# Turning the activations between two layers: from TensorE's transposes to VectorE's 32x32 blocks and GpSimd's transfers

## The chip, the cores and the metric

The kernel runs on one core of a Trainium2 chip. The metric is the device time of one execution in microseconds (us); the time before is the median of three executions. One execution was also recorded by the hardware profiler, and all rows shown here come from such recordings.

## The reference

Two layers, each a mixer over 256 tokens of width 2048, followed by a residual and a layer norm. Cut to what matters here:

```python
def hybrid_layer(x, mem, w_in, ..., w_mem_kv, w_out, ln_g, ln_b):
    h = x @ w_in                        # (256, 2048) @ (2048, 6672)
    a_q, a_k, a_v, a_z, b_q, b_k, b_v, b_z, b_lr, m_q, m_z = split(h)
    y_a = chunk_band_attention(a_q, a_k, a_v, rel_table)
    y_b = gla_chunk_recurrence(b_q, b_k, b_v, gates(b_lr)) ...
    mk, mv = split(mem @ w_mem_kv)      # keys and values of 256 memory tokens
    y_m = memory_attention(m_q, mk, mv)
    y = concatenate([y_a * silu(a_z), y_b * silu(b_z), y_m * silu(m_z)])
    return layer_norm(DEEPNORM_ALPHA * x + y @ w_out, ln_g, ln_b)

def reference(...):
    h = x
    for l in range(2):
        h = hybrid_layer(h, mem, w_in[l], ..., ln_g[l], ln_b[l])
    return h
```

The output of layer 0, normed, is the `x` of layer 1. The products need it with the model dimension on the partitions (turned), since TensorE sums over partitions. The residual of layer 1 needs it with the tokens on the partitions (not turned).

## The kernel before

**Products.** A group of columns of a weight matrix is computed by `as_group`: eight pieces of weights (128 x 2 x 512 float32, 512 KB), and for each piece twelve matmuls (two blocks of 128 model rows, two halves of the tokens, three products). Each float32 operand is split in two parts that TensorE takes at full rate: `parts` has ScalarE cast the high part (`hi`, line 128) and VectorE subtract it to get the low part (`lo`, line 129). For a block and a half, `as_products` multiplies in this order: high activations by high weights, low activations by high weights, high activations by low weights. The activations are the operand that is loaded into the array (LDWEIGHTS), the weights stream.

**Buffers.** `piece` takes its buffers `raw`, `wh` and `wl` from a ring of four: piece n+4 goes into the place of piece n. The turned activations lie in four quarters `xq[0..3]`, each an `operand()` of 128 x 4 blocks x (high, low) x 256 tokens, from a ring of five; quarter q serves the pieces 2q and 2q+1 of a group.

**Order.** TensorE, SyncE and GpSimd run in the order in which the program is written. For ScalarE and VectorE a scheduler decides the order when the kernel is built: the casts of weight pieces have a high priority (`tc.high_priority(AHEAD)`), and `placed_here` keeps an instruction where the program has it relative to its neighbours. Work that is to lie between the products is a Python generator: `tick()`, called after each piece, advances those in `active` and `side`; an entry of `side` starts at a given tick.

**Between the layers.** `norm_between` norms the whole output of layer 0, `res` (128 tokens x 2 halves x 2048), in place without gain and bias: ScalarE takes the column blocks 0 and 2, VectorE 1 and 3 (four instructions each). Meanwhile TensorE runs the first group of layer 1, the values of the memory (called MV here), which does not need `res`. Then comes the group of the memory's keys (MK), also without `res`, and then the queries and keys of the linear attention (BQK), the first group on the new activations; after it the first group of values (V). `transposed`, a generator that is run during MK, turns `res`: eight times four transposes of 128 x 128 on TensorE into a PSUM bank, a gain and bias per model row on the way out (ScalarE one block, VectorE the other), and `parts`. The gain and bias come turned as well: `norm_columns` loads them as 32 rows, and one transpose turns these into `gbT`. `restored` later applies gain and bias to `res` itself for the residual.

**Turning without TensorE.** The kernel has another way, `turned`, used for attention operands: VectorE transposes each 32 x 32 block in place of a 128 x 512 tile (line 525), GpSimd writes the tile to a buffer `home` in device memory (line 527), and four reads per tile (line 532) bring the blocks to their partitions. The reads are put on GpSimd's queue two ticks later.

Of the kernel before, what the change touches and what calls it, by code (L numbers as in the profile page):

```python
# [8 lines left out]
F32 = mybir.dt.float32  # L9
# [3 lines left out]
AF = mybir.ActivationFunctionType  # L13
ALU = mybir.AluOpType
# [4 lines left out]
P = 128  # L19
D = 2048  # L20
T = 256
# [11 lines left out]
AHEAD = 4000  # L33
# [3 lines left out]
def hybrid_trunk_kernel(  # L37
# [7 lines left out]
    pe, dve, act, pool, sp = nc.tensor, nc.vector, nc.scalar, nc.gpsimd, nc.sync  # L45
# [4 lines left out]
    waiting, active, side, done, now, linear = [], [], [], set(), [0], []  # L50

    def tick(share=1.0):

        now[0] += share
        for e in [e for e in side if e[1] <= now[0]]:
            side.remove(e)
            after = next(e[0], None)
            if after is not None:
                side.append((e[0], now[0] + after))
            else:  # L60
                done.add(e[0])
        while True:
            while waiting and len(active) < (3 if all(g in done for g in linear) else 2):
                active.append((waiting.pop(0), 0))
            due = [e for e in active if e[1] <= now[0]]
            if not due:
                return
            active.remove(due[0])
            g = due[0][0]
            after = next(g, None)  # L70
            if after is not None:
                active.append((g, now[0] + after))
                return
            done.add(g)

    def finish(gens):
        while not all(g in done for g in gens):
            tick()

    def enter(name, bufs=1, **kw):  # L80
        return ctx.enter_context(tc.tile_pool(name=name, bufs=bufs, **kw))
# [5 lines left out]
    hd = enter("hd", 1)  # L87
# [5 lines left out]
    drm = enter("drm", 6, space=bass.MemoryType.DRAM)  # L93
# [3 lines left out]
    def nm(s):  # L97
        uid[0] += 1
        return f"{s}_{uid[0]}"
# [4 lines left out]
    def bank():  # L104
        return psa.tile([P, 512], F32, name=nm("bk"), tag="bk")

    def scratch(shape, dtype=F32):
        return sc.tile(shape, dtype, name=nm("sc"), tag="sc")
# [4 lines left out]
    ident = cst.tile([P, P], F32, name="ident")  # L113
# [3 lines left out]
    def operand():  # L117

        x = opp.tile([P, 4, 2, T], F32R, name=nm("x"), tag="x")
        return x[:, :, 0], x[:, :, 1], x.rearrange("p j h t -> p j (h t)")  # L120
# [5 lines left out]
    def parts(hi, lo, src, keep=lambda ins: ins):  # L126

        keep(act.copy(hi, src))  # L128
        keep(dve.tensor_tensor(lo, src, hi.bitcast(F32), op=ALU.subtract))  # L129
# [477 lines left out]
        act.copy(y, po[:, :256])  # L607
        yield 2

    def transposed(xq, gbT):  # L610

        raw, gT = gbT
        pt = bank()
        pe.transpose(pt[:, :P], raw, ident)
        dve.tensor_copy(gT, pt[:, :32])
        for q in range(4):
            x = operand()
            hi, lo, _ = x
            xq.append(x)
            for j in range(0, 4, 2):  # L620
                pt = bank()
                y = scratch([P, 2, T])
                for jj in range(2):
                    kt = q * 4 + j + jj
                    for t in range(2):
                        pe.transpose(pt[:, jj * T + t * P:jj * T + (t + 1) * P], res[:, t, kt * P:(kt + 1) * P], ident)  # L626
                with tc.high_priority(AHEAD // 4):
                    for jj in range(2):
                        kt = q * 4 + j + jj
                        src, g, b = pt[:, jj * T:(jj + 1) * T], gT[:, kt:kt + 1], gT[:, 16 + kt:17 + kt]  # L630
                        if jj == 0:
                            act.activation(y[:, jj], src, AF.Identity, bias=b, scale=g)
                        else:
                            dve.tensor_scalar(y[:, jj], src, g, b, op0=ALU.mult, op1=ALU.add)
                    parts(hi[:, j:j + 2], lo[:, j:j + 2], y)
                yield 1

    def restored(gb):

        for n in range(WO_N):  # L640
            for t in range(2):
                r = res[:, t, columns(n)]
                tc.keep_in_program_order(dve.tensor_tensor(r, r, gb[n][0], op=ALU.mult))
                dve.tensor_tensor(r, r, gb[n][1], op=ALU.add)
                yield 2

    def columns(n):
        return slice(n * 512, (n + 1) * 512)
# [31 lines left out]
    def norm_columns(l):  # L680

        raw = hd.tile([P, P], F32, name=nm("gbrow"), tag="pairs0")
        pool.memset(raw, 0.0)
        for i, src in enumerate((ln_g, ln_b)):
            pool.dma_start(raw[i * 16:i * 16 + 16], src[l].rearrange("(k p) -> k p", p=P))
        return raw, hd.tile([P, 32], F32, name=nm("gbT"), tag="pairs1")

    def norm_rows(l, rows):

# [104 lines left out]
    res = per.tile([P, 2, D], F32, name="res")  # L794
# [3 lines left out]
    for l in range(L):  # L798
# [15 lines left out]
        xq = []  # L814
        if l == 0:
            def each(p):
                if p in (2, 4, 6, 7):
                    xq.append(resident_quarter(len(xq), xT[len(xq)]))

            raw = hd.tile([P, 4, T], F32, name=nm("qk"), tag="qk", bufs=4)  # L820
            laid_out(first_memory(mv, each), raw, lambda src, at: parts(at(mk[0]), at(mk[1]), src, placed_here))
        else:
            memq = []
            parts(*mv, as_group(w512[l, G_MV], memq, 512, 2, memT))
            gens = [transposed(xq, gbT), restored(gb)]
            waiting.append(gens[0])
            raw = hd.tile([P, 4, T], F32, name=nm("qk"), tag="qk", bufs=4)
            mkey = staged(G_MK, memq, raw, lambda src, at: parts(at(mk[0]), at(mk[1]), src, placed_here))
            finish(gens[:1])

        gq = hd.tile([P, 2, T], F32, name=nm("gq"), tag="gq")
        gk = hd.tile([P, 2, T], F32, name=nm("gk"), tag="gk")
        raw = hd.tile([P, 4, T], F32, name=nm("qk"), tag="qk", bufs=4)
# [7 lines left out]
        qk = scratch([P, 2, 256])  # L841
# [2 lines left out]
        dg = small([P, 8], "ms")  # L844
        dve.tensor_reduce(dg, qk.rearrange("p t (h d) -> p (t h) d", d=64), AX.X, ALU.add)
        if l > 0:
            waiting.append(gens[1])
        gp = gla_inputs(l)
        if l == 0:
            sp.dma_start(ident, ident_d)  # L850
# [20 lines left out]
        blocks = scratch([P, 2, 64])  # L871
        dve.transpose(blocks.rearrange("p b (t j) -> p t b j", j=32), lr[:, :, :64].bitcast(F32).rearrange("p t (b j) -> p t b j", j=32))
        home = drm.tile([P, 2, 64], F32, name=nm("home"), tag="home64")
# [15 lines left out]
        bias = {}  # L889
# [11 lines left out]
        gens = [[gla(*gp, gq, gk, lrT, dg, asv, yraw)]]  # L901
# [12 lines left out]
        for half in range(2):  # L914
            q, k = (hd.tile([P, 4, T], F32, name=nm("qk"), tag="qk", bufs=4) for _ in range(2))
# [43 lines left out]
        gb = []  # L959
# [8 lines left out]
        for n in range(WO_N):  # L968
# [3 lines left out]
            src = wo_pieces(l, n)  # L972
            if last and n == WO_N - 1:
# [3 lines left out]
                rest = bank()[:, :256]  # L977
# [39 lines left out]
        if not last:  # L1017
            for n in range(WO_N):
                both = per.tile([P, 2, 512], F32, name=nm("gb"), tag=f"yr{n}")
                gb.append((both[:, 0], both[:, 1]))  # L1020
                load_norm(n)
            norm_between(stats)
            gbT = norm_columns(l)


# [84 lines left out]
```

## Time and profile before

| | |
|---|---|
| median of 3 executions | 900.3 us (900.08 to 900.83) |
| the profiled execution's own time | 900.78 us |
| its span in the trace | 899.0 us |
| granted TensorE clock, mean | 0.998 |
| TensorE busy | 891.3 us (99%) |
| VectorE, ScalarE, GpSimd busy | 611.8, 478.6, 214.4 us |
| transfers | 213.74 MB, mean 238 GB/s |

The profiled execution's time lies 1.8 us over its span; these 1.8 us lie around the span and are not touched by the change. A timeline row has the start in us from the span's start, the length in us, the engine, the line of the kernel, the operation with output and input, and the count; behind it in brackets the time that the engine sat idle before it and what ended that. Rows with a count above 1 merge neighbours; one instruction's length overlaps the next one's start on an engine, so the cost of an instruction on a busy engine is the distance between starts.

### The profile page before, as it was taken

Reading aid. Unit: us, or ns where it says so; the run is one execution under the profiler, and the core shown is the slowest. Engines: PE = TensorE matmul, PEld = TensorE weight load, DVE = VectorE, ACT = ScalarE, POOL = GpSimd, SP = SyncE. Lnnn points to the kernel's source line nnn. Section 1 sums busy time; section 2 is a strip of 40 time slices with the busy share of each in tenths; the row PEclk is TensorE's granted clock in tenths of the full one; section 3 lists DMA queues with packets and bytes.
Section 4 is the critical chain, followed back from the end, with each engine's and each line's share of the span. In section 5 each row is a group of like instructions: output and inputs, shape, how many; then the busy total and the mean of one; then the engine's idle time right before and its main releaser. Section 6 shows DMA issues by size and latency. Waiting matters only on the chain.

```text
span 899.0 us, 13806 instructions
## 1 busy us (share of the span) xinstructions
PE 891.3 (99%) x4687; PEld 746.6 (83%) x4687; DVE 611.8 (68%) x887; ACT 478.6 (53%) x686; POOL 214.4 (24%) x401
## 2 busy tenths in 40 slices
PE   9999999999999999999999999999999999999997
PEld 7888988888988888888888888888888888888885
DVE  6756568767477667665587777796565767676766
ACT  6644575555445566544476444854744457565440
POOL 0022103115315443410000221231061344433200
PEclk9999999999999999999999999999999999999999
DMA  8887779867989797975675859697479897979762
GB/s 309 310 260 226 231 235 268 262 207 220 275 254 241 236 271 238 316 236 188 227 241 184 233 164 286 195 292 213 150 224 296 244 270 221 287 217 289 218 183 94
DMA packets 164838, 213.74 MB, mean 238 GB/s; under 512 B 24752, under 2 KB 142896, under 8 KB 164768
## 3 DMA queue, kind: packets, MB, share of 16 engines
q1 hardware_dynamic: 148256, 173.29, 63.4%
q0 software_dynamic: 16224, 39.18, 15.2%
q8 instruction: 37, 0.61, 0.3%
q10 hardware_dynamic: 288, 0.39, 0.1%
q14 instruction: 33, 0.27, 0.1%
HBM read 193.20 MB, written 19.53 MB: 237 GB/s over the span
## 4 chain that ended last, share of the span: by engine, by line
PE 98%; DMA 1%; DVE 0%; ACT 0%; SPq 0%; issue 0%
PE acc L102 91%; PE bk L102 6%; DMA raw<-w 1%; PE bk L626 0%; ACT res L784 0%; SPq L179 0%; ACT wh L128 0%; DVE stats L770 0%; DVE res L769 0%; SPq L203 0%; SPq L201 0%; DVE res L720 0%; DVE mvt L723 0%; PE bk L773 0%; ACT nparts L774 0%
## 5 line engine op out<-in xcount | busy, mean ns | idle before, releaser
L102 PE MATMUL acc<-wh,x 128*128 128x512 f32 (+2 forms) x2516 | 749.4, 381 | 0.4 <-ACT wh L128 0.2
L102 PEld LDWEIGHTS acc<-wh,x 128*128 128x128 f32 x2516 | 460.7, 188 | 87.0 <-ACT wh L128 1.3
L129 DVE TENSOR_TENSOR wl<-raw,wh 128x1024 fp32r<-128x1024 f32 (+3 forms) x321 | 368.2, 1151 | 209.5 <-ACT wh L128 204.9
L128 ACT CAST wh<-raw 128x1024 fp32r<-128x1024 f32 (+3 forms) x321 | 318.7, 996 | 346.6 <-PE acc L102 212.8
L102 PE MATMUL acc<-wl,x 128*128 128x512 f32 (+2 forms) x1258 | 476.6, 379 | 0.0
L102 PEld LDWEIGHTS acc<-wl,x 128*128 128x128 f32 x1258 | 236.2, 188 | 45.6 <-DVE wl L129 1.1
L527 POOL DMA_DIRECT2D home<-sc x70 | 39.2, 560 | 458.1 <-DVE sc L525 442.6
L532 POOL DMA_DIRECT2D pT<-home x96 | 52.5, 553 | 28.5 <-DMA home<-sc 12.8
L532 POOL DMA_DIRECT2D qk<-home x64 | 34.9, 553 | 30.4 <-DMA home<-sc 28.5
L532 POOL DMA_DIRECT2D zT<-home x48 | 26.2, 552 | 21.8 <-DMA home<-sc 14.0
L525 DVE STREAM_TRANSPOSE sc<-sc 128x512 f32<-128x512 f32 (+1 forms) x38 | 24.9, 667 | 3.7 <-ACT sc L950 3.0
L532 POOL DMA_DIRECT2D yr<-home x48 | 26.3, 555 | 3.2 <-DMA home<-sc 3.2
L525 DVE STREAM_TRANSPOSE sc<-acc 128x512 f32<-128x512 f32 x28 | 18.3, 691 | 5.0 <-PE acc L102 4.8
L554 ACT ACTIVATE sc<-sc,mx 128x128 f32<-128x128 f32 (+1 forms) x32 | 14.4, 449 | 13.0 <-DVE mx L552 13.0
L547 DVE SCALAR_TENSOR_TENSOR sc<-bk,bias 128x384 f32<-128x384 f32 x16 | 8.6, 538 | 10.7 <-PE bk L102 10.7
L128 ACT CAST x<-sc 128x512 fp32r<-128x512 f32 x20 | 12.3, 617 | 5.0 <-DVE sc L508 3.8
L129 DVE TENSOR_TENSOR x<-sc,x 128x512 fp32r<-128x512 f32 x20 | 13.7, 685 | 1.4 <-ACT x L128 1.4
L102 PEld LDWEIGHTS bk<-pT,asv 128*128 128x128 f32 x64 | 11.8, 189 | 1.8
L102 PE MATMUL bk<-qk,qk 128*128 128x128 f32 (+1 forms) x64 | 13.1, 326 | 0.0
L102 PE MATMUL bk<-pT,asv 128*128 128x256 f32 (+1 forms) x64 | 13.0, 326 | 0.0
L659 DVE SCALAR_TENSOR_TENSOR res<-res,acc 128x512 f32<-128x512 f32 x15 | 9.7, 681 | 4.0 <-PE acc L102 4.0
L129 DVE TENSOR_TENSOR x<-raw,x 128x1024 fp32r<-128x1024 f32 x5 | 6.1, 1226 | 8.9 <-ACT x L128 8.8
(204 smaller groups left out, 506.4 us busy)
## 6 DMA issues: line engine op xcount, KB each, us to landing
raw<-w SPq DMA_DIRECT2D x387, 256.0 KB, 4.7
raw<-w SPq DMA_DIRECT2D x62, 512.0 KB, 4.9
home<-sc POOLq DMA_DIRECT2D x54, 256.0 KB, 4.3
raw<-w SPq DMA_DIRECT2D x32, 388.0 KB, 5.1
raw<-w SPq DMA_DIRECT2D x32, 264.0 KB, 3.3
qk<-home POOLq DMA_DIRECT2D x64, 64.0 KB, 5.2
raw<-w SPq DMA_DIRECT2D x32, 124.0 KB, 4.8
bias<-relw SPq DMA_DIRECT2D x16, 192.0 KB, 4.6
```

The costliest lines, as they stand in the source:

```text
L102: pe.matmul(o, l, r, start=start, stop=stop, skip_group_check=True)
L128: keep(act.copy(hi, src))
L129: keep(dve.tensor_tensor(lo, src, hi.bitcast(F32), op=ALU.subtract))
L525: dve.transpose(blocks.rearrange(order, j=32), src.rearrange("p (g b j) -> p g b j", b=4, j=32))
L527: pool.dma_start(homes[-1], blocks)
L532: pool.dma_start(dst[b * 32:(b + 1) * 32], home[:, b].rearrange("(a i) n -> i a n", a=4))
L547: dve.scalar_tensor_tensor(s, pb[:, :384], SCALE, bias[h], op0=ALU.mult, op1=ALU.add)
L554: act.activation(s[:, own[t]], s[:, own[t]], AF.Exp, bias=mx[:, t:t + 1], accum_out=zs[:, t:t + 1])
L659: dve.scalar_tensor_tensor(r, r, ALPHA, acc, op0=ALU.mult, op1=ALU.add)
```

## The change

`transposed` is gone, and with it all 32 transposes of `res` and the one of the gain and bias on TensorE. Right after `norm_between`, four calls of `turned` bring the whole of `res` through VectorE's blocks and `home` buffers to four tiles `xT`: eight block transposes on VectorE, eight writes and thirty-two reads on GpSimd's queue. `norm_columns` turns the gain and bias in the same way, with one block transpose, one write and four reads, while the output projection of layer 0 still runs. A new generator `landed` takes the place of the rest of `transposed`: gain and bias, now read from `xT`, then `parts`. It is put on `side` six ticks after MV's end, one step per tick, two steps to a quarter, with all its instructions `placed_here` and without the raised priority. The program no longer finishes the generator before BQK.

```diff
-    def transposed(xq, gbT):
-
-        raw, gT = gbT
-        pt = bank()
-        pe.transpose(pt[:, :P], raw, ident)
-        dve.tensor_copy(gT, pt[:, :32])
-        for q in range(4):
-            x = operand()
-            hi, lo, _ = x
-            xq.append(x)
-            for j in range(0, 4, 2):
-                pt = bank()
-                y = scratch([P, 2, T])
-                for jj in range(2):
-                    kt = q * 4 + j + jj
-                    for t in range(2):
-                        pe.transpose(pt[:, jj * T + t * P:jj * T + (t + 1) * P], res[:, t, kt * P:(kt + 1) * P], ident)
-                with tc.high_priority(AHEAD // 4):
-                    for jj in range(2):
-                        kt = q * 4 + j + jj
-                        src, g, b = pt[:, jj * T:(jj + 1) * T], gT[:, kt:kt + 1], gT[:, 16 + kt:17 + kt]
-                        if jj == 0:
-                            act.activation(y[:, jj], src, AF.Identity, bias=b, scale=g)
-                        else:
-                            dve.tensor_scalar(y[:, jj], src, g, b, op0=ALU.mult, op1=ALU.add)
-                    parts(hi[:, j:j + 2], lo[:, j:j + 2], y)
-                yield 1
+    def landed(x, xT, q, gT):
+
+        hi, lo, _ = x
+        xv = xT.rearrange("p t a (k j) -> p k t a j", j=32)
+        for j in range(0, 4, 2):
+            y = scratch([P, 2, T])
+            for jj in range(2):
+                kt = q * 4 + j + jj
+                src, g, b = xv[:, j + jj], gT[:, kt:kt + 1], gT[:, 16 + kt:17 + kt]
+                o = y[:, jj].rearrange("p (t a j) -> p t a j", t=2, j=32)
+                if jj == 0:
+                    placed_here(act.activation(o, src, AF.Identity, bias=b, scale=g))
+                else:
+                    placed_here(dve.tensor_scalar(o, src, g, b, op0=ALU.mult, op1=ALU.add))
+            parts(hi[:, j:j + 2], lo[:, j:j + 2], y, placed_here)
+            yield 1
...
-        return raw, hd.tile([P, 32], F32, name=nm("gbT"), tag="pairs1")
+        gT = hd.tile([P, 32], F32, name=nm("gbT"), tag="pairs1")
+        blocks = scratch([P, 4, 32])[:32]
+        dve.transpose(blocks, raw[:32].rearrange("p (b j) -> p b j", j=32))
+        home = drm.tile([32, 4, 32], F32, name=nm("home"), tag="home32")
+        pool.dma_start(home, blocks)
+        for b in range(4):
+            pool.dma_start(gT[b * 32:(b + 1) * 32], home[:, b])
+        return gT
...
             parts(*mv, as_group(w512[l, G_MV], memq, 512, 2, memT))
-            gens = [transposed(xq, gbT), restored(gb)]
-            waiting.append(gens[0])
+            gens = [restored(gb)]
+
+            def rest():
+                for q, xT in turns.items():
+                    xq.append(operand())
+                    yield from landed(xq[q], xT, q, gbT)
+
+            side.append((rest(), now[0] + 6))
             raw = hd.tile([P, 4, T], F32, name=nm("qk"), tag="qk", bufs=4)
             mkey = staged(G_MK, memq, raw, lambda src, at: parts(at(mk[0]), at(mk[1]), src, placed_here))
-            finish(gens[:1])
...
             norm_between(stats)
             gbT = norm_columns(l)
+            turns = {}
+            for q in range(4):
+                turns[q] = hd.tile([P, 2, 4, P], F32, name=nm("xT"), tag="qk", bufs=4)
+                turned(P, *((turns[q][:, t], res[:, t, columns(q)]) for t in range(2)))
```

How this moves instructions shows at two places. The first is VectorE between the layers, at the end of MV. In the kernel before, `wl_4399` is the low part of MV's last piece, and `wl_4421`, `wl_4454`, `wl_4483` those of MK's pieces 0, 1 and 2:

```order
L678 TENSOR_SCALAR res<-res,rstd_4220,nmr_4221 128x512 x4
L129 TENSOR_TENSOR wl_4399<-raw_4397,wh_4398 128x1024
L129 TENSOR_TENSOR wl_4421<-raw_4419,wh_4420 128x1024
L129 TENSOR_TENSOR wl_4454<-raw_4452,wh_4453 128x1024
L129 TENSOR_TENSOR wl_4483<-raw_4481,wh_4482 128x1024
```

The same place in the changed kernel, where `wl_4475` is the low part of MV's last piece and `wl_4497` that of MK's piece 0:

```order
L667 TENSOR_SCALAR res<-res,rstd_4220,nmr_4221 128x512 x4
L129 TENSOR_TENSOR wl_4475<-raw_4473,wh_4474 128x1024
L525 STREAM_TRANSPOSE sc_4255<-res 128x4x4x32
L525 STREAM_TRANSPOSE sc_4259<-res 128x4x4x32
L525 STREAM_TRANSPOSE sc_4264<-res 128x4x4x32
L525 STREAM_TRANSPOSE sc_4268<-res 128x4x4x32
L525 STREAM_TRANSPOSE sc_4273<-res 128x4x4x32
L525 STREAM_TRANSPOSE sc_4277<-res 128x4x4x32
L525 STREAM_TRANSPOSE sc_4282<-res 128x4x4x32
L525 STREAM_TRANSPOSE sc_4286<-res 128x4x4x32
L129 TENSOR_TENSOR wl_4497<-raw_4495,wh_4496 128x1024
```

All eight block transposes now stand between the low parts of MV's last piece and of MK's first.

The second place is ScalarE in BQK. In the kernel before, `x_4618` is the last quarter of the activations (each cast fills one half of it), `sc_4649` what the gain and bias of its second half made, and `wh_4736`, `wh_4755`, `wh_4774`, `wh_4793`, `wh_4812` are the high parts of BQK's pieces 3 to 7:

```order
L128 CAST wh_4736<-raw_4735 128x1024
L128 CAST x_4618<-sc_4620 128x2x256
L632 ACTIVATE sc_4649<-bk_4648,gbT_4245 128x256
L128 CAST wh_4755<-raw_4754 128x1024
L128 CAST x_4618<-sc_4649 128x2x256
L128 CAST wh_4774<-raw_4773 128x1024
L128 CAST wh_4793<-raw_4792 128x1024
L128 CAST wh_4812<-raw_4811 128x1024
```

In the changed kernel `x_4727` is the third quarter and `x_4776` the last; `wh_4807`, `wh_4826` and `wh_4845` are BQK's pieces 5, 6 and 7, and `wh_4893` and `wh_4918` the pieces 0 and 1 of the next group, V:

```order
L128 CAST wh_4807<-raw_4806 128x1024
L621 ACTIVATE sc_4728<-xT_4272,gbT_4245 128x256
L621 ACTIVATE sc_4752<-xT_4272,gbT_4245 128x256
L128 CAST wh_4826<-raw_4825 128x1024
L128 CAST x_4727<-sc_4728 128x2x256
L128 CAST x_4727<-sc_4752 128x2x256
L128 CAST wh_4845<-raw_4844 128x1024
L128 CAST wh_4893<-raw_4892 128x1024
L128 CAST wh_4918<-raw_4917 128x1024
L621 ACTIVATE sc_4777<-xT_4281,gbT_4245 128x256
L621 ACTIVATE sc_4801<-xT_4281,gbT_4245 128x256
L128 CAST x_4776<-sc_4777 128x2x256
```

The cast of the last quarter's first half has moved from behind the weight cast of BQK's piece 3 to behind that of V's piece 1, six weight casts later.

More of the change, by code (lines that the diff above doesn't have):

```diff
@@ L846, in hybrid_trunk_kernel @@
         if l > 0:
-            waiting.append(gens[1])
+            waiting.append(gens[0])
         gp = gla_inputs(l)
```

## The prediction

> **What bounds the kernel now.** I read the page first: its busy times (part 1) and the chain of work that ended last (part 4).
>
> ```profile
> PE 891.3 (99%) x4687; PEld 746.6 (83%) x4687; DVE 611.8 (68%) x887; ACT 478.6 (53%) x686; POOL 214.4 (24%) x401
> PE 98%; DMA 1%; DVE 0%; ACT 0%; SPq 0%; issue 0%
> ```
>
> TensorE is the bound. Then the waits of TensorE, in whole:
>
> ```profile
> PE bk L102 <- DVE eps L797: 1.1, 1, 1.1
> PE bk L773 <- DVE nt L738: 0.9, 1, 0.9
> PE bk L102 <- ACT nparts L774: 0.3, 1, 0.3
> PE acc L102 <- ACT wh L128: 0.2, 1, 0.2
> ```
>
> The first is the start of the kernel, the next two its end, so between the ends TensorE never waits for anybody. Two things follow: every matmul taken out shortens the kernel by its place on TensorE, and every wait put into the middle lengthens it in full. VectorE and ScalarE have time to spare in sum; what counts is whether one operand is late at one moment.
>
> **What is removed.** The timeline of TensorE around the transposes:
>
> ```profile
> 467.20 0.62 PE L102 MATMUL acc<-wh,x 128*128 128x512 f32 x2
> 467.65 0.39 PE L102 MATMUL acc<-wl,x 128*128 128x512 f32 x1
> ...
> 469.92 0.27 PE L614 MATMUL bk<-ident,gbrow 128*128 128x128 f32 x1
> 470.03 0.60 PE L626 MATMUL bk<-ident,res 128*128 128x128 f32 x4
> ...
> 473.23 0.60 PE L626 MATMUL bk<-ident,res 128*128 128x128 f32 x4
> 473.59 0.71 PE L102 MATMUL acc<-wh,x 128*128 128x512 f32 x2
> ...
> 495.72 0.62 PE L102 MATMUL acc<-wh,x 128*128 128x512 f32 x2
> ...
> 498.44 0.61 PE L102 MATMUL acc<-wh,x 128*128 128x512 f32 x2
> ...
> 509.32 0.62 PE L102 MATMUL acc<-wh,x 128*128 128x512 f32 x2
> ```
>
> MK starts at 467.20, and its third matmul, the first that takes a low weight part, at 467.65. A piece without transposes takes 498.44 - 495.72 = 2.72 us. From 469.92 to 495.72 lie eight pieces and all 33 transposes: 25.80 - 8 x 2.72 = **4.04 us** that go. A lower bound counts only the four transposes' own places, 473.59 - 473.23 = 0.36 us: 8 x 0.36 + 0.11 = 2.99 us. I take 4.04, since the pieces between are slower (their matmuls follow at a slightly larger distance) than those outside.
>
> The Trainium skill, page VectorE: DVE Perf Modes, section Rules for kernel authors, speaks against the change: a 128x128 transpose belongs on TensorE where a PSUM destination will do, with 390 ns for it. Worked out from that page, an estimate of the gain would be 33 x 0.39 = 12.9 us; the trace disagrees, since 33 cost 4.04 us there.
>
> **What is added on VectorE: a wait at MK's first piece.** VectorE and ScalarE at the end of MV, and the distance between two block transposes elsewhere:
>
> ```profile
> 459.67 1.92 DVE L678 TENSOR_SCALAR res<-res,rstd,nmr 128x512 f32<-128x512 f32 x4
> 461.50 1.22 DVE L129 TENSOR_TENSOR wl<-raw,wh 128x1024 fp32r<-128x1024 f32 x1
> 463.57 3.50 DVE L129 TENSOR_TENSOR wl<-raw,wh 128x1024 fp32r<-128x1024 f32 x3 [0.86 <-ACT wh L128]
> ```
>
> ```profile
> 459.67 2.93 ACT L676 ACTIVATE res<-res,nmr,rstd 128x512 f32<-128x512 f32 x4
> ```
>
> ```profile
> 359.86 1.31 DVE L525 STREAM_TRANSPOSE sc<-sc 128x512 f32<-128x512 f32 x2 [0.69 <-ACT sc L950]
> 361.09 0.72 DVE L508 TENSOR_TENSOR sc<-zT,yr 128x256 f32<-128x256 f32 x2
> ```
>
> Before, the low parts of MK's pieces 0 to 2 start at 463.57. Now the eight block transposes come first. They can start when MV's last low part is through, 461.50 + 1.22 - 0.08 of overlap = 462.64 (the norm's last block is done at 459.67 + 2.93 = 462.60). Two took 361.09 - 359.86 = 1.23 us, so eight take 4.92, to 467.56; the low part takes 1.22, to 468.78. TensorE wants it at 467.65. The wait sits at the load of the activations that goes with this matmul, and that load is then no longer hidden:
>
> ```profile
> L102 PEld LDWEIGHTS acc<-wh,x 128*128 128x128 f32 x2516 | 460.7, 188 | 87.0 <-ACT wh L128 1.3
> ```
>
> With its 0.19 the matmul starts at 468.97: a wait of **1.3 us**, 1.1 without the load. Queued behind the transposes are also the low parts of pieces 1 to 3; each takes 1.2 against TensorE's 2.72, so they catch up. SyncE's refill of the raw ring starts up to 4 us later, and lands within
>
> ```profile
> DMA to landing us min/median/max: 2.7/4.5/9.8
> ```
>
> in the median 4.5 us (min, median and max of the loads of weight pieces), at about 474, while MK's piece 4 is due at 467.20 + 1.3 + 4 x 2.72 = 479.4. At the longest landing, 9.8, piece 4 would be about 1.5 us late; I count nothing and keep this for the range.
>
> **What is added on GpSimd: hidden.** Its queue gets 8 writes, then 32 reads.
>
> ```profile
> 366.99 4.36 POOL L532 DMA_DIRECT2D zT<-home  x8 [3.75 <-DMA home<-sc]
> ...
> 373.72 0.55 POOL L963 DMA_DIRECT2D gb<-ln_g  x1 [1.25 <-DMA zT<-home]
> ```
>
> ```profile
> home<-sc POOLq DMA_DIRECT2D x54, 256.0 KB, 4.3
> zT<-home POOLq DMA_DIRECT2D x48, 64.0 KB, 5.8
> ```
>
> Eight reads are issued in 4.36 us, and a further transfer then waited for an old one to land, so I take 5.8 + 0.5 us per eight. The last block transpose ends at 467.6; its write is issued by 468.2 and lands 4.3 later, at 472.5. The first quarter's last read follows and lands by 479, the others 6.3 us apart: 485, 491, 498. ScalarE asks for the first when MK's piece 7 is cast, near 480, and BQK needs it at 467.20 + 1.3 + 8 x 2.72 = 490.3. The fourth is asked for near 508. Everything lands in time, with 6 us or more to spare for TensorE. MK's own turning is queued behind these reads on GpSimd, but starts only at 490.
>
> The gain and bias are turned during layer 0's output projection, where VectorE idles about 1.5 us per piece and is three pieces ahead: nothing, and at worst under 1 us.
>
> **What is moved on ScalarE: a wait in BQK.** The cast of the last quarter now stands behind that of V's piece 1. When is that one made?
>
> ```profile
> 489.27 1.05 ACT L128 CAST wh<-raw 128x1024 fp32r<-128x1024 f32 x1 [1.18 <-PE acc L102]
> 490.22 0.61 ACT L128 CAST x<-sc 128x512 fp32r<-128x512 f32 x1
> 490.74 0.56 ACT L632 ACTIVATE sc<-bk,gbT 128x256 f32<-128x256 f32 x1
> ...
> 509.30 1.06 ACT L128 CAST wh<-raw 128x1024 fp32r<-128x1024 f32 x1 [1.15 <-PE acc L102]
> ```
>
> ```profile
> 491.49 0.69 DVE L129 TENSOR_TENSOR x<-sc,x 128x512 fp32r<-128x512 f32 x1
> ```
>
> The ring has four places, so V's piece 1 takes that of BQK's piece 5 and is cast when TensorE is through with it: the row at 509.30, where BQK's piece 6 starts at 509.32. Piece 6 is the first that needs the last quarter. So when TensorE reaches piece 6, ScalarE begins: the cast 0.95 (490.22 - 489.27), two gain-and-bias instructions 0.47 each (0.56 less the 0.09 by which rows overlap), the quarter's high cast 0.61: 2.5 us. Then VectorE's low part 0.69, and 0.19 for the load: the second matmul starts 3.4 us after the first should have, against 0.23 normally. A wait of **3.2 us**; 2.6 if low part and loads were hidden, 3.6 with 0.1 for each handover. The third quarter has the same form, but stands behind the cast of BQK's piece 6, which is made at the end of piece 2; its low part is ready 0.95 + 0.61 + 1.23 + 0.05 = 2.84 us later, and TensorE wants it 2.72 + 0.23 = 2.95 later, load included: **0.1 us**, at most 0.3.
>
> **The sum.** -4.04 + 1.3 + 0.1 + 3.2 = +0.6 us on the profiled execution's 900.78, which is 901.4; that execution lies 0.48 over the median of 900.3, so the forecast is **900.9 us**. With the bounds of the terms it runs from -4.04 + 1.1 + 2.6 = -0.3 to -2.99 + 1.4 + 0.3 + 3.6 = +2.3, 900.0 to 902.6. What can be told from no change here is about 0.2%, 1.8 us; below 898.5 is faster, above 902.1 slower.
>
> **The rivals.** *The clock falls in the wait (slower).* The timeline of TensorE at the end of the kernel, and busy times in short stretches (the number after POOL's is the granted clock):
>
> ```profile
> 893.54 0.39 PE L102 MATMUL bk<-gbrow,nparts 8*128 8x512 f32 x1
> ```
>
> ```profile
> 893.00:894.00 1.00, 0.94 (x3) 0.45 (x3) 0.75 (x3) 0.50 (x1) 0.00 (x0) 1.00 0.37 131
> 895.70:895.90 0.20, 0.00 (x0) 0.00 (x0) 0.00 (x0) 0.00 (x0) 0.00 (x0) 1.00 1.04 389
> 895.90:896.10 0.20, 0.00 (x0) 0.00 (x0) 0.00 (x0) 0.00 (x0) 0.00 (x0) 0.81 1.02 399
> 896.10:896.30 0.20, 0.00 (x0) 0.00 (x0) 0.00 (x0) 0.00 (x0) 0.00 (x0) 0.50 0.98 369
> ```
>
> The last matmul ended at 893.93; the clock fell to half at about 896.0, after 2.1 us of rest. The wait in BQK is longer, broken by one matmul. If the clock falls there, the work after it runs at half speed for a while; the trace shows 3.0 us of it (896.0 to 899.0, its end), which costs 1.5 us of work: 900.9 + 1.5 = 902.4. It decides from 2.4 us of half clock. For it: the 2.1 us. Against: such a fall came once, and the waits of 0.9 and 0.3 us before it did nothing. The Trainium skill, page TensorE: Matmul & The Clock Gate, Part 1, says that the clock is halved after one idle window of about 3.4 us and comes back after a busy one; by that rule a wait of 3.2 us with a matmul in it would mostly pass, and the trace, with 2.1 us, does not agree on the length. By its window an estimate of the loss is 1.7 us. Chance 0.27.
>
> *The transfers are late (slower).* Eight writes of 256 KB and 32 reads of 64 KB, 4.2 MB, are added within 30 us. It decides when the first quarter lands after 486, or a weight piece comes 3.5 us over the median; each us beyond costs one: 902 to 906, about 904. Against it: the median landings leave 6 us. Chance 0.14.
>
> *The wait in BQK is not there (faster).* If the first use of the last quarter were hidden, the sum is -4.04 + 1.3 + 0.1 = -2.6: 897.7; without any wait 896.3. For it: the transfers are in time; against: one queue in order, and the ring of four as the rows show. Chance 0.09.
>
> **How the numbers follow.** My case has 0.50, all of it within 0.2%. Of the clock's 0.27 I put 0.20 above 902.1 and 0.07 below; of the late transfers' 0.14, 0.13 above; of the last 0.09, 0.08 below 898.5. Faster 0.08, same 0.59, slower 0.33. The range 898.9 to 903.5 leaves out most of the last rival and the late transfers' upper half, about 0.15.
>
> **What would show it.** In the changed kernel's trace: no L614 or L626 on TensorE and MK in 21.8 us plus its wait; a first wait of TensorE for VectorE's `wl` of about 1.3 us near 467.7; a second for ScalarE's and VectorE's `x` of about 3.2 in sum near 506.6; ScalarE asking for `xT` after it has landed. A clock below 1.00 near 510, a wait on a transfer, or a sum of waits under 2.2 us would prove me wrong.

## The result: slower, and the profile after

| | before | after |
|---|---|---|
| median of 6 executions | 900.52 us (900.08 to 901.99) | 907.22 us (905.64 to 907.73) |
| ratio, 95% interval | | 1.0071 (1.0060 to 1.0081) |
| the profiled execution, its span | 900.78, 899.0 us | 905.64, 903.5 us |

The changed kernel is 6.7 us slower. The profiled execution is the fastest of the six, so the rows below account for 4.9 us and not for all 6.7.

The page of the changed kernel, busy times and the chain that ended last:

```profile
PE 890.0 (99%) x4654; PEld 743.7 (82%) x4654; DVE 614.3 (68%) x895; ACT 478.7 (53%) x686; POOL 238.5 (26%) x446
PE 92%; DMA 4%; DVE 1%; ACT 1%; issue 0%; POOL 0%; SPq 0%; ACTq 0%; DVEq 0%
```

The 33 transposes are gone (x4687 to x4654 on TensorE), but 4% of the chain is now a transfer, where it was 1%. The waits of TensorE, and its timeline in BQK:

```profile
PE acc L102 <- ACT x L128: 3.0, 2, 2.5
PE acc L102 <- DVE x L129: 2.6, 3, 1.8
```

```profile
494.56 0.51 PE L102 MATMUL acc<-wh,x 128*128 128x512 f32 x1 [0.48 <-ACT x L128]
496.83 0.50 PE L102 MATMUL acc<-wh,x 128*128 128x512 f32 x1 [1.76 <-DVE x L129]
...
503.19 0.50 PE L102 MATMUL acc<-wh,x 128*128 128x512 f32 x1 [0.62 <-DVE x L129]
...
508.32 0.39 PE L102 MATMUL acc<-wl,x 128*128 128x512 f32 x1
511.19 0.50 PE L102 MATMUL acc<-wh,x 128*128 128x512 f32 x1 [2.48 <-ACT x L128]
511.91 0.51 PE L102 MATMUL acc<-wh,x 128*128 128x512 f32 x1 [0.23 <-DVE x L129]
512.25 0.39 PE L102 MATMUL acc<-wl,x 128*128 128x512 f32 x1
...
513.34 1.05 PE L102 MATMUL acc<-wh,x 128*128 128x512 f32 x2
```

All waits in the middle are for `x`, the turned activations, and they stand at BQK's pieces 2, 4 and 6, the first that need the second, third and last quarter. Measured by the distance of the low-weight matmuls (0.68 us when nothing waits; at the last quarter 512.25 - 508.32 - 0.68), they cost 2.8, 0.9 and 3.25 us, loads included. Then two matmuls take 1.05 us where two take 0.62. The clock, in short stretches (the third number from the end is the granted clock):

```profile
513.00:516.50 3.50, 3.50 (x10) 2.73 (x9) 0.06 (x1) 0.79 (x1) 0.00 (x0) 0.52 0.46 147
516.50:520.00 3.50, 3.50 (x17) 2.86 (x16) 2.75 (x4) 1.41 (x3) 0.00 (x0) 1.00 0.15 22
```

Half the clock for 3.5 us: 3.5 x 0.48 = 1.7 us of work. Together with the 4.0 us that the transposes took, 2.8 + 0.9 + 3.25 + 1.7 - 4.0 = +4.6, against 4.9 measured.

Why the quarters are late begins with the transfers. Transfers issued between 460 and 490, first of before, then of after (count, size, median us to landing):

```profile
raw<-w SPq DMA_DIRECT2D x23, 256.0 KB, 3.5
```

```profile
raw<-w SPq DMA_DIRECT2D x20, 256.0 KB, 7.4
home<-sc POOLq DMA_DIRECT2D x8, 256.0 KB, 4.3
xT<-home POOLq DMA_DIRECT2D x27, 64.0 KB, 6.3
```

The turning transfers landed as fast as forecast, but a weight load takes twice as long beside them. That fits the Trainium skill, page DMA: Bandwidth & Descriptors, section Issuing engines are not separate DMA queues: transfers of all issuing engines end on the same 16 DMA engines and interleave there. ScalarE's waits for the loads of weights between 455 and 520, before and after:

```profile
ACT wh L128 <- DMA raw<-w: 0.4, 1, 0.4
```

```profile
ACT wh L128 <- DMA raw<-w: 17.2, 10, 6.6
```

ScalarE and VectorE of the changed kernel around the second quarter (L621 and L623 are the gain and bias, L128 and L129 the high and low parts):

```profile
490.89 1.05 ACT L128 CAST wh<-raw 128x1024 fp32r<-128x1024 f32 x1 [2.01 <-DMA raw<-w]
491.85 0.60 ACT L621 ACTIVATE sc<-xT,gbT 128x256 f32<-128x256 f32 x1
492.66 1.05 ACT L128 CAST wh<-raw 128x1024 fp32r<-128x1024 f32 x1 [0.22 <-DMA raw<-w]
493.89 0.62 ACT L128 CAST x<-sc 128x512 fp32r<-128x512 f32 x1 [0.18 <-ACT wh L128]
494.42 0.60 ACT L621 ACTIVATE sc<-xT,gbT 128x256 f32<-128x256 f32 x1
495.13 0.62 ACT L128 CAST x<-sc 128x512 fp32r<-128x512 f32 x1
```

```profile
493.44 1.30 DVE L525 STREAM_TRANSPOSE sc<-acc 128x512 f32<-128x512 f32 x2
494.67 0.37 DVE L623 TENSOR_SCALAR sc<-xT,gbT 128x256 f32<-128x256 f32 x1
494.96 1.22 DVE L129 TENSOR_TENSOR wl<-raw,wh 128x1024 fp32r<-128x1024 f32 x1
496.10 1.28 DVE L129 TENSOR_TENSOR x<-sc,x 128x512 fp32r<-128x512 f32 x2
```

The quarter's steps stand behind the casts of weight pieces that wait for their loads, and on VectorE behind two block transposes of MK's result. Its low part is begun at 496.1; TensorE wanted it at 494. No instruction of ScalarE or VectorE waits for a transfer of `xT` in this trace: what is late is not the quarter's landing.

### The profile page after: what moved, and what is told of

Same layout as the page of the kernel before. It is cut to its first block, busy times and chain, and to the rows that moved or that the text cites. A ratio compares the mean times of both kernels' runs of the same rounds, so it can differ in the third digit from the quotient of the medians.

```text
span 903.5 us, 13841 instructions
## 1 busy us (share of the span) xinstructions
PE 890.0 (99%) x4654; PEld 743.7 (82%) x4654; DVE 614.3 (68%) x895; ACT 478.7 (53%) x686; POOL 238.5 (26%) x446
## 4 chain that ended last, share of the span: by engine, by line
PE 92%; DMA 4%; DVE 1%; ACT 1%; issue 0%; POOL 0%; SPq 0%; ACTq 0%; DVEq 0%
PE acc L102 86%; PE bk L102 6%; DMA raw<-w 4%; DVE wl L129 1%; DMA qk<-home 1%; ACT wh L128 1%; POOL qk L532 0%; ACT sc L621 0%; SPq L153 0%; ACT res L780 0%; ACT asv L862 0%; DVE x L129 0%; ACT x L128 0%; DVE stats L766 0%; DVE res L765 0%
## 5 line engine op out<-in xcount | busy, mean ns | idle before, releaser
L129 DVE TENSOR_TENSOR wl<-raw,wh 128x1024 fp32r<-128x1024 f32 (+3 forms) x321 | 368.0, 1151 | 211.6 <-ACT wh L128 209.9
L128 ACT CAST wh<-raw 128x1024 fp32r<-128x1024 f32 (+3 forms) x321 | 318.7, 996 | 353.4 <-PE acc L102 209.9
L527 POOL DMA_DIRECT2D home<-sc x78 | 43.5, 559 | 418.7 <-DVE sc L525 409.9
L532 POOL DMA_DIRECT2D xT<-home x32 | 17.5, 552 | 11.2 <-DMA xT<-home 5.0
L129 DVE TENSOR_TENSOR x<-sc,x 128x512 fp32r<-128x512 f32 x20 | 13.4, 684 | 1.0 <-ACT x L128 1.0
L128 ACT CAST x<-sc 128x512 fp32r<-128x512 f32 x20 | 12.1, 617 | 2.9 <-DVE sc L508 2.6
```

What stands on the lines that cost most here:

```text
L527: pool.dma_start(homes[-1], blocks)
L532: pool.dma_start(dst[b * 32:(b + 1) * 32], home[:, b].rearrange("(a i) n -> i a n", a=4))
```

## Theories and experiments

There are four theories. T1: the transfers delay the weight loads, and late weights hold up TensorE. T2: the order on ScalarE and VectorE alone makes the waits. T3: TensorE's rest lowers the clock and adds to each wait. T4: transfers and order together. Every time is a median; every ratio is against the kernel before on the same chip (medians 900.6 to 900.7 us), with its 95% interval. The ratio is not the quotient of the medians; the two differ by up to 0.1%. The edits are cut to what matters: `...` and `<...>` stand for what is left out.

**1. The transfers without the change.**

```diff
+ home = drm.tile([P, 4, P], ...); pool.dma_start(home, res[:, t, columns(q)]...)   # 8 writes
+ pool.dma_start(dst[b * 32:(b + 1) * 32], home[:, b]...)                           # 32 reads, unused
```

> The kernel before, which turns its quarters on TensorE as it did, with the 40 transfers of the changed kernel (8 writes of 256 KB to device memory, 32 reads of 64 KB back into tiles that nobody uses) added to GpSimd's queue. It leaves nothing out. T1 (the transfers slow the weight loads, whose casts then come late and hold up everything queued behind them): the median landing of a weight piece between 460 and 490 rises from 3.5 us towards the 7.4 of the changed kernel, ScalarE waits for weights for 5 us or more where it waited 0.4 us before, and TensorE waits in BQK for 0.5 to 3.5 us: 901 to 904 us. T2 alone (only the order on ScalarE and VectorE matters): the landings may rise, but the time stays at 900.5 within 0.5. T3 (the clock) adds 1.7 us only if a wait of 2 us or more comes up.

901.2 us, ratio 0.9999 (0.9990 to 1.0008). The loads are as late as feared, and ScalarE waited 17.8 us for weights, yet TensorE waited for nothing in BQK:

```profile
raw<-w SPq DMA_DIRECT2D x20, 256.0 KB, 8.5
```

```profile
490.00:500.00 10.00, 10.00 (x49) 8.30 (x48) 8.62 (x12) 7.26 (x12) 4.92 (x9) 1.00 1.10 270
```

Late weights alone cost nothing that can be measured: the casts were ahead by more than the delay. T1 alone falls, for a TensorE that still makes its transposes.

**2. The change without the bytes.**

```diff
- pool.dma_start(homes[-1], blocks)
+ pool.dma_start(home[:, 0, :8], dst[:, 0, :8])     # the reads cut in the same way
```

> The changed kernel with its 40 transfers kept in number and order, but cut to 8 columns each (a thirty-second or less of the bytes); the block transposes write straight into the tiles that are read. Left out: the move of blocks between partitions, so what BQK and later groups multiply is not the layer's input. T1: with the bytes gone the weight pieces land after 3.5 to 4.5 us again and the waits in BQK's pieces 2 and 4 (2.7 and 0.8 us) go. T2: the last quarter still stands behind the cast of V's piece 1 on ScalarE, so a wait of 2 to 3.2 us stays at BQK's piece 6, and by T3 another 1.7 us of low clock behind it: 900.5 - 4.0 + (0 to 1.3 at MK) + 3.1 + (0 to 1.7) = 899.6 to 902.6. If the late landing of V's piece 1 (1.7 us of ScalarE's wait) was part of that wait, it falls to 1.4 us without a clock loss: 897.9 to 899.2. If the order alone makes all the waits (T2 for pieces 2 and 4 too): 905 to 907.

901.2 us, ratio 0.9998 (0.9990 to 1.0007). The weights land nearly as soon as in the kernel before:

```profile
raw<-w SPq DMA_DIRECT2D x24, 256.0 KB, 4.0
```

The timeline of TensorE has three waits in MK and BQK:

```profile
467.68 0.50 PE L102 MATMUL acc<-wl,x 128*128 128x512 f32 x1 [0.58 <-DVE wl L129]
...
507.05 0.51 PE L102 MATMUL acc<-wh,x 128*128 128x512 f32 x1 [1.43 <-ACT x L128]
508.39 0.50 PE L102 MATMUL acc<-wh,x 128*128 128x512 f32 x1 [0.84 <-DVE x L129]
```

These are MK's wait and piece 6's; those at pieces 2 and 4 are gone (a wait of 0.48 us comes later, at 548). The order costs what the transposes save; the bytes bring the other 6 us, though by themselves they cost nothing. So the two act together (T4).

**3. TensorE kept busy in the waits.**

```diff
+ if pc in fill: for i in range(fill[pc]): mm(spare, mv[0][:, 0, :P], mv[0][:, 0], ...)   # {2: 8, 6: 10}
```

> The changed kernel with 8 matmuls ahead of BQK's piece 2 and 10 ahead of its piece 6 in layer 1, into a bank that nobody reads: about 0.227 us each, so 1.8 and 2.3 us, laid into waits of 2.7 and 3.1 us. T3 (TensorE's rest is what lowers the clock): the granted clock stays at 0.95 or more between 510 and 520, and the time falls by 1.5 to 1.7 us to about 905.5. If the clock falls for another reason, or the rest that is left is enough for it: 907 to 907.5, or up to 0.5 more where a wait is shorter than its filling.

904.0 us, ratio 1.0033 (1.0019 to 1.0047): with 4.1 us more work it is 3.2 us faster than the changed kernel's 907.2, twice what T3 expected. The clock stayed up where the changed kernel's fell:

```profile
510.00:515.00 5.00, 5.00 (x24) 4.14 (x23) 2.52 (x3) 2.67 (x5) 0.00 (x0) 1.00 1.10 321
```

T3 holds in direction. For the size the record has the mean granted clock of each execution: on average 0.9955 over the changed kernel's six and 0.998 over these nine, an estimate of at most 2.4 us of work (0.0026 x 905). So the clock can make most of the 3.2 us on average, but not execution by execution: 907.73 us came with 0.997, the profiled 905.64 us with 0.995. The rest of the size is not settled.

**4. The last quarter ahead of V's casts.** Only ScalarE's and VectorE's order is bound.

```diff
+ tc.add_manual_dep(<cast of V's piece 0>, <cast of the last quarter>, NoSync)   # and the low parts
```

> The changed kernel with one bound on the order: on ScalarE and on VectorE the casts of V's pieces 0 and 1 stand behind those of the last quarter. T2 (the last quarter waits for nothing but its place behind the cast of V's piece 1): the wait of 3.1 us at BQK's piece 6 goes, and by T3 the low clock behind it (1.7 us): about 902.4. Without T3 (a clock that falls anyway) about 904. T1 alone (the late weights hold up whatever stands there): the wait moves to V's pieces 0 and 1, 1.5 to 3 us, and the time is 904.5 to 907. In all of these the waits at BQK's pieces 2 and 4 stay at about 2.7 and 0.8.

903.1 us, ratio 1.0028 (1.0017 to 1.0038). No wait at piece 6 is left; those at piece 2 stay (1.76 and 1.78 us), and in this profile, of an execution of 905.0 us, the clock falls behind them, to 0.50 from 500 to 505. The order was piece 6's cause. In the kernels with a bound order lines are shifted: L103 is the matmul, L632 and L634 are the gain and bias, L129 both parts.

```profile
499.80 0.80 PE L103 MATMUL acc<-wh,x 128*128 128x512 f32 x1 [1.78 <-DVE x L129]
```

**5. All three quarters earlier.** The casts of BQK's pieces 2, 5 and 7 stand behind the second, third and last quarter (5b: pieces 3, 6, 7; 5c: 5 with tiny transfers).

```diff
+ acc = as_group(halves(G_BQK), xq, 512, behind={2: 1, 5: 2, 7: 3})
```

> The changed kernel with three bounds on the order of ScalarE and VectorE: the cast of BQK's piece 2 stands behind those of the second quarter, that of piece 5 behind the third quarter's, that of piece 7 behind the last quarter's. The transfers are untouched. T4 (transfers and order together: late weights alone cost nothing, as the transfers added to the kernel before showed, and the order alone costs 2.6 us, as the tiny transfers showed; the waits at pieces 2 and 4 come because a quarter's casts stand behind a later weight piece that lands late): the waits at pieces 2, 4 and 6 go and the clock stays at 1.00, which leaves 900.6 - 4.0 + 0.2 to 0.6 at MK + up to 0.5 elsewhere = 896.8 to 897.7, faster than the kernel before. T1 alone (late weights hold up TensorE in any order): the waits move to the low parts or casts of weight pieces, 1 to 3 us with or without a fall of the clock: 898 to 902. T2 alone would also give 897, but says that the time is the same with tiny transfers.

> As the one before, but with less lead: the second quarter only ahead of piece 3's cast, the third only ahead of piece 6's, the last ahead of piece 7's. T4: the second quarter still stands behind the cast of piece 2, the piece that it is used with, and the third behind that of piece 5; a late weight piece then shows for a part of the time: waits of 0 to 1.5 us at pieces 2 and 4 and nothing at 6, 897 to 900 us, and no faster than the one with more lead. T1 alone: no difference to that one.

> The tiny transfers (8 columns each; the move of blocks between partitions left out, so that BQK and the later groups multiply other numbers) with the same three bounds as the kernel with the quarters first. T2 and T4: no wait at pieces 2, 4 and 6, MK's 0.2 to 0.6: 896.6 to 897.3. The difference between the two is what the bytes of the transfers cost where the casts have lead: by T4 under 0.5 us, by T1 alone 1.5 us or more.

Measured: 901.1 us, ratio 1.0003 (0.9992 to 1.0013); 5b 901.7, 1.0011 (1.0002 to 1.0020); 5c 898.6, 0.9974 (0.9963 to 0.9985). My T4 figure of 897 for the first failed, 5b lies above its 897 to 900, and 5c came 1.3 us higher than expected, with 0.72 us of wait at MK. TensorE in kernel 5:

```profile
497.13 0.73 PE L103 MATMUL acc<-wh,x 128*128 128x512 f32 x2 [2.14 <-ACT wh L129]
498.39 0.50 PE L103 MATMUL acc<-wl,x 128*128 128x512 f32 x1 [0.53 <-DVE wl L129]
```

The wait at piece 2 has moved from `x` to the weights, as T1 said. But are the weights late, or are they held?

> The changed kernel once more, on the chip of the three before. 906.8 to 907.7 us. If the profile falls on a run nearer to its median than the first one (905.6, the fastest of six), it shows the waits in BQK longer by 1 to 2 us together, or a second stretch of low clock, about 1.7 us more.

907.9 us, ratio 1.0073 (1.0059 to 1.0087). Its profile is again of an execution below the median (905.7 us), so what the usual one loses beyond that stays open.

**6. The same bytes, needed by nobody.**

```diff
+ pool.dma_start(home, dst)                          # full size
+ pool.dma_start(unused[...], home[:, b]...)         # instead of xT; quarters straight from the blocks
```

> The kernel with the quarters first, with its 40 transfers at full size and in their place on GpSimd's queue, but into memory that nobody reads: the quarters are taken straight from the block transposes (left out: the move of blocks between partitions, so BQK and the later groups multiply other numbers). So the weight loads meet the same traffic, TensorE turns nothing, and no cast waits for a turned quarter. TA (the bytes make the weight pieces late, and TensorE, with no transposes between its pieces, asks for a piece every 2.72 us where it asked every 3.21 us in the kernel before, so it catches up with them): waits of TensorE on wh or wl or behind them of 1.5 to 3.5 us, 900 to 902 us. TB (what is late is the landing of the turned quarters, not the weights): no wait beyond MK's 0.2 to 0.7, 898.2 to 899.2 us as with tiny transfers.

899.0 us, ratio 0.9978 (0.9967 to 0.9988). The weights are as late as ever, and TensorE hardly notices:

```profile
raw<-w SPq DMA_DIRECT2D x20, 256.0 KB, 8.2
```

```profile
495.02 0.73 PE L103 MATMUL acc<-wh,x 128*128 128x512 f32 x2 [0.21 <-ACT wh L129]
496.28 0.51 PE L103 MATMUL acc<-wl,x 128*128 128x512 f32 x1 [0.53 <-DVE wl L129]
```

Bytes against tiny transfers (5c): 0.4 us, within the intervals. TA falls. The quarters are also cast earlier here, so landing and order were still not apart.

**7 and 8. Fewer quarters by transfer.** Quarters 0 and 1 (7), or quarter 0 alone (8), and the norm's rows go through TensorE as before.

```diff
- for q in range(4): turns[q] = ...; turned(...)
+ for q in range(K, 4): ...                # and transposed() for q < K, K = 2 or 1
```

> Quarters 0 and 1 and the norm's rows are turned by TensorE as in the kernel before, quarters 2 and 3 by VectorE's blocks and GpSimd's transfers, with the casts of BQK's piece 5 behind quarter 2 and of piece 7 behind quarter 3. 16 of 33 transposes go (-1.96 us at 4.04/33 each) and 20 of 40 transfers stay (2.1 of 4.2 MB moved twice). If the waits come from the traffic against a faster TensorE, half of both leaves next to none: 898.6 to 899.4. By TB too, since the quarters that are used first do not depend on transfers: 898.6 to 899.2. If any traffic at this place costs its share: 899.5 to 900.5.

> Quarter 0 and the norm's rows by TensorE, quarters 1 to 3 by blocks and transfers, with the casts of BQK's pieces 2, 5 and 7 behind quarters 1, 2 and 3. 24 of 33 transposes go (-2.94 us), 30 of 40 transfers stay. TA: waits of 0 to 2.5 us, 897.8 to 900.5, more than with two quarters each way. TB: the transfers of quarter 1 now start first and it lands some 7 us earlier, so no waits: 897.7 to 898.4.

899.3 us, ratio 0.9982 (0.9973 to 0.9991), and 899.7, 0.9980 (0.9971 to 0.9990): both faster than both kernels, and with no wait of TensorE in MK or BQK. Kernel 8 has one of 0.65 us in V, and lies above the 897.7 to 898.4 that TB gave it.

**9. The second quarter ahead of piece 1 as well.**

```diff
- behind={2: 1, 5: 2, 7: 3}
+ behind={1: 1, 4: 2, 6: 3}
```

> The changed kernel with the quarters first and one step more: the second quarter's casts stand ahead of the cast of BQK's piece 1, not only of piece 2's. In the run with the quarters first, the second quarter's last read was issued by 481 and landed some 6.4 us later, at about 488, but ScalarE came to it at 490.7, after the cast of piece 1, which waited for its weights until 489.8; piece 2's cast stood behind both, and TensorE waited 2.1 and 0.5 us for it. If the order is what is left of the loss: the second quarter is cast at 488 to 490, the wait at piece 2 falls under 1 us, the clock stays at 1.00, and the time is 898.6 to 899.8. If the landing of the turned quarter is what is left: piece 1's cast now waits behind the quarter, the wait moves to piece 1 with the same 2 to 2.7 us, the clock falls behind it, and the time stays at 900.6 to 901.6.

903.0 us, ratio 1.0025 (1.0015 to 1.0036). That is above both expected ranges. By the wait, which moved to piece 1, the landing would be what is left. The rows say otherwise:

```profile
488.39 0.60 ACT L632 ACTIVATE sc<-xT,gbT 128x256 f32<-128x256 f32 x1
490.32 0.62 ACT L129 CAST x<-sc 128x512 fp32r<-128x512 f32 x1 [1.33 <-DVE sc L634]
490.85 0.60 ACT L632 ACTIVATE sc<-xT,gbT 128x256 f32<-128x256 f32 x1
493.28 0.62 ACT L129 CAST x<-sc 128x512 fp32r<-128x512 f32 x1 [1.83 <-DVE sc L634]
493.80 2.94 ACT L129 CAST wh<-raw 128x1024 fp32r<-128x1024 f32 x3
```

```profile
494.89 1.22 PE L103 MATMUL acc<-wh,x 128*128 128x512 f32 x2 [2.74 <-ACT wh L129]
```

No step waits for a transfer. ScalarE waits twice for VectorE inside the quarter, and three weight pieces, then cast in a row without a wait, stood behind it. What I had bound was a slow sequence.

**10 and 11. A quarter's steps in one go.** First both scales on each engine, then both casts; MK's block transposes then fall behind the second quarter. Number 11 is the same with quarter 0 by TensorE.

```diff
- for j in (0, 2): scale(j); scale(j + 1); parts(...); yield 1
+ scale(0), scale(1), scale(2), scale(3); parts(...); parts(...); yield 1
+ behind={1: 1, 4: 2, 7: 3}
```

> The changed kernel with the second, third and last quarter ahead of the casts of BQK's pieces 1, 4 and 7, and with a quarter's steps in one go: both scales on each engine first, then both casts, and MK's two block transposes no longer between them. The transfers are untouched. If the steps were what was late (in the run before, the second quarter had landed by 487.2 but its steps ran from 488.4 to 494.6, with 3.2 us of them ScalarE waiting for VectorE): the quarter is done by 492, the waits fall to 0 to 1.2 us together with no fall of the clock, and the time is 897.5 to 899. If the landing is what is late: 901 to 903 as before, with ScalarE or VectorE waiting for a transfer of xT.

> The same with quarter 0 and the norm's rows turned by TensorE as in the kernel before (24 transposes removed, -2.94 us; 30 transfers stay). With the steps in one go the 1.6 us of waits that the earlier kernel with three turned quarters showed fall to under 1: 897.8 to 898.8. If landings decide: 899 to 900, no better than before.

Number 10: 899.3 us, ratio 0.9986 (0.9978 to 0.9995). Number 11: 899.4, 0.9985 (0.9975 to 0.9994). Against number 9, number 10 changes more than the order within a quarter: the program puts a quarter in one step and not in two, and the last quarter stands ahead of piece 7's cast and not of piece 6's. ScalarE and TensorE of number 10:

```profile
488.71 1.09 ACT L632 ACTIVATE sc<-xT,gbT 128x256 f32<-128x256 f32 x2
490.63 1.14 ACT L129 CAST x<-sc 128x512 fp32r<-128x512 f32 x2 [0.83 <-DVE sc L634]
491.68 1.99 ACT L129 CAST wh<-raw 128x1024 fp32r<-128x1024 f32 x2
...
496.21 1.09 ACT L632 ACTIVATE sc<-xT,gbT 128x256 f32<-128x256 f32 x2 [0.95 <-DMA xT<-home]
```

```profile
492.78 0.73 PE L103 MATMUL acc<-wh,x 128*128 128x512 f32 x2 [0.27 <-ACT wh L129]
494.04 0.50 PE L103 MATMUL acc<-wl,x 128*128 128x512 f32 x1 [0.53 <-DVE wl L129]
```

The quarter is cast by 491.8, two us sooner than in number 9, and the same transfers, all still needed, now belong to a kernel that is 8 us faster than the changed one. One step does wait for a transfer, which the expectation had named as the sign of a late landing: the third quarter's gain and bias, 0.95 us. TensorE does not wait behind it. So the second quarter's landing was not the bound; place and length of the quarters' steps were, though which of number 10's changes counted is not shown.

Number 10 came slightly above the 897.5 to 899 expected. Number 11's 899.4 lies in the band that its expectation gave to late landings, but its trace shows none: no step waits for a transfer, and TensorE has no wait in MK or BQK, only one of 1.08 us for a low weight part in V. Kernels 7, 8, 10 and 11 are 0.14% to 0.20% faster than before and cannot be told apart. Of the 4 us that the transposes cost, 1.0 to 1.3 us (by the medians) or 1.3 to 1.8 us (by the ratios) was won; in number 10's profile the distances of the low-weight matmuls still show 1.9 us lost in MK and BQK.

## Why the prediction was wrong, step by step

- **The failed step: "What is added on GpSimd: hidden", with the late refill of weights, "I count nothing".** I checked that the turned quarters land in time, and they did. I did not ask what 4.2 MB do to the weight loads on the same DMA engines, beyond their old spread: the median went from 3.5 to 7.4 us, and ScalarE's waits for weights from 0.4 to 17.2 us. Late weights alone would still have cost nothing (1). But in the new order the quarters' steps stand behind the casts that wait for them, and the lead that I used as cover was gone: together 6 us (2).
- **The second quarter was left out.** I costed the third (0.1 us) and the last (3.2 us) with weights always at hand. With late ones the second cost 2.8 us and the third 0.9. The tiny transfers show both terms near nothing once the weights are in time.
- **BQK's piece 6, 3.2 us: right.** 3.25 measured; gone when only the order was bound (4). In the second profile TensorE holds the cast of V's piece 1, as forecast (ScalarE waits 1.66 us for it). In the first it is the load of that piece (1.73 us), which landed at about the same moment: that the size fits there too is luck.
- **MK's first piece, 1.3 us: oversized.** Neither profile of the changed kernel shows it; over the variants it was 0 to 1.28 us, mostly 0.3 or less. The norm ended earlier relative to TensorE than in the profile of before, for a reason that stays open: in the changed kernel the block transposes began at 460.75, not at 462.64.

```profile
457.79 1.92 DVE L667 TENSOR_SCALAR res<-res,rstd,nmr 128x512 f32<-128x512 f32 x4
...
460.75 4.85 DVE L525 STREAM_TRANSPOSE sc<-res 128x512 f32<-128x512 f32 x8
```

- **The clock rival happened**, on top of the forecast: 1.7 us for 3.5 us of half clock, where I had 1.5 for 3.0.
- **The rival of late transfers** came nearest in time (about 904), but its two points did not decide: the first quarter was in time, and a weight piece 4 us over the median cost nothing by itself (1). It needed the order as well.
- **The transposes, -4.04 us: about right.** The gaps that they leave between the low-weight matmuls of before sum to 3.7 us. The 390 ns that the prediction took from the Trainium skill, page VectorE: DVE Perf Modes, stand there under The three transpose paths and for bfloat16; these transposes are float32.

Without its bytes the changed kernel takes 901.2 us (2), close to the 900.9 forecast: the steps of the sum were sound for everything but what the transfers do to others. That the total fits so well is partly luck: in that profile MK's first piece costs 0.74 us against 1.3 and piece 6 2.8 against 3.2, and a wait of 0.48 us at 548 was not forecast.

## What to carry to other kernels

Before an off-path transfer is called hidden, ask what it does to the loads that share the DMA engines with it, and how far ahead of use those loads' consumers stand on each in-order engine. Late loads are harmless as long as nothing urgent is queued behind their casts; place what TensorE needs next ahead of work that may wait for a load, and keep its steps together so that two engines do not wait for each other by turns. A rest of TensorE in mid-kernel is to be priced at its length plus a possible fall of the clock.

## What the runs showed of the hardware

The same rest lowers the clock in one execution and not in another. In the second profile of the changed kernel TensorE waited 0.96 and 1.77 us at piece 2 and 2.42 and 0.23 us at piece 6:

```profile
499.00:500.00 1.00, 1.00 (x4) 0.81 (x3) 0.86 (x1) 0.00 (x0) 0.00 (x0) 0.50 1.13 331
500.00:502.50 2.50, 2.50 (x8) 1.93 (x8) 1.33 (x2) 2.19 (x4) 0.00 (x0) 0.60 1.03 365
...
513.00:516.50 3.50, 3.01 (x12) 2.29 (x13) 1.90 (x3) 1.26 (x3) 0.00 (x0) 1.00 0.94 300
```

Here the clock fell behind the first and stayed at 1.00 behind the second; in the first profile it was the other way round. Shorter rests do it too: in 5b 0.83 and 0.91 us with a matmul between them were followed by a clock of 0.50 from 499 to 502, while in kernel 2 the clock stayed at 1.00 behind 1.43 and 0.84 us. The Trainium skill, page TensorE: Matmul & The Clock Gate, Part 1, has the clock judged in windows of about 3.4 us that run freely, whenever the work starts; the low stretch of 3.5 us and this lottery agree with that. The section also asks for a whole idle window before the clock falls; that was not needed here, since a matmul lay within each of these rests.
